# Attention's value products: two matmuls per key tile instead of three, and denominators from GpSimd sums

## The chip, the core and the metric

The kernel runs on one core of a Trainium2 chip. The core has a matrix engine (TensorE, called PE in the rows, with its weight loads as PEld), VectorE (DVE), ScalarE (ACT), GpSimd (POOL) and SyncE (SP, which issues DMAs). Each engine works through its own list of instructions in a fixed order. The metric is the time of one execution in microseconds; the profile shows one such execution, instruction by instruction.

## What is computed

One layer: a gated feed-forward block, then a mixer (attention beside a short convolution), then a second gated feed-forward block, for 1024 latent tokens and 256 context tokens with a model width of 1024. The change touches only the attention of the mixer, 8 query heads in 2 groups of 4 that share a key and value head of width 64:

```
def gqa_softmax(q, k, v):
    s = jnp.einsum('bqkgd,bskd->bkgqs', q, k, preferred_element_type=jnp.float32) * ATTN_SCALE
    p = jax.nn.softmax(s, axis=-1).astype(v.dtype)
    return jnp.einsum('bkgqs,bskd->bqkgd', p, v)
...
    k_all = jnp.concatenate([kc, k], axis=1)
    v_all = jnp.concatenate([vc, v], axis=1)
```

Every latent query reads 1280 keys: 1024 latent ones and 256 of the context. All inputs are float32.

## The kernel before

The program has three parts: the first feed-forward block with its loads (to about 770 us), the projections and attention (to about 1470 us), and the second feed-forward block. A scheduler puts every engine's instructions in order when the program is built, following the order of the code and the buffers that come free.

**Precision.** A float32 number is carried as a high part (rounded to the matrix engine's faster float32 type, `F32R`) and a low part, the rest. ACT writes the high part (a cast), DVE writes the low part (a subtraction of two tensors). A product of two such pairs is three matmuls: high by high, high by low, low by high.

**Attention.** The loop at L1564 goes over 16 pairs `gi` of a 128-query tile and a head group. For each of them `back` (L1403) goes over 10 key tiles `kt` of 128 keys. `st_exp` (L1325) makes one tile's scores for 4 heads x 128 queries (two matmuls into `pT`, L1330 and L1331) and their exponentials `pexp` (ACT, L1333). For the eight latent key tiles (`SPLIT`, L896) it then makes the high part (ACT, L1343) and the low part (DVE, L1344); for the two context tiles (`UNSPLIT`) it keeps the float32 tile. Three key tiles later (`LAG`, L1410) `tp_v` (L1347) multiplies by the values into a PSUM tile `pvo` of 128 rows: rows 0 to 63 are the sums of p times v, and rows 64 to 127 are the softmax denominator, since the right half of `v_hi` and `v_f` holds ones. A latent tile takes three matmuls (L1353, L1354, and L1355 with the low values from `vlq`, into 64 rows), and a context tile one float32 matmul (L1350), which the profile records as two matmuls.

After the tenth key tile `attn_end` (L1366) is stepped through during the next pair: ACT copies the denominators to `rcs` (L1372), DVE takes reciprocals (L1375) and multiplies (L1380), and squares are summed for the norm that follows.

**Beside it** run the steps of `front` for the next pair: score matmuls `s__` (L1307) whose row maxima DVE reduces out of PSUM (L1308), and `smax_end` (L1310), in which POOL makes a diagonal tile `dgm` (L1315) and copies queries (L1321). The fill generators `fill_pe` (L1258) and `fill_dve` (L1280) add the second half of the mixer's projections and the convolution's work in fixed proportions.

**Buffers.** Tiles tagged `t2` (128x512, six of them) hold `pexp`, some of the parts, and most temporaries. Three buffers tagged `raw` take weights from DMA until ACT and DVE have split them (L277). PSUM has 4 banks `in`, 3 banks `o` and 1 bank `m` (L88).

Of the kernel before, what the change touches and what calls it, by code (L numbers as in the profile page):

```python
# [6 lines left out]
F32 = mybir.dt.float32  # L7
# [20 lines left out]
def layer_kernel(  # L28
# [876 lines left out]
    def v_of(k):  # L905
        n = SPLIT.index(k)
        if k >= 8:
            return v_c[:, n - NVA, :, 0:P], v_c[:, n - NVA, :, P:P + HD]
        return vt["hi"][:, n], vt["lo"][:, n]

    vt = {}

# [59 lines left out]
    def make_v(pt, N, k0):  # L972
        vf = t2("vf", [P, N])
        act.copy(vf, pt)
        nt = N // P
        pv = ps("o", [P, nt, P], "pvt")
        for t in range(nt):
            pe.transpose(pv[:, t, :], vf[:, t * P:(t + 1) * P], ident)
        one = ones1.unsqueeze(2).to_broadcast([P, 2, HD])
        for t in range(nt):  # L980
            k = k0 + t
            src = pv[:, t, :].rearrange("p (g d) -> p g d", g=2)
            if k in SPLIT:
                v, vl = v_of(k)
                act.copy(v[:, :, 0:HD], src)
                dve.tensor_tensor(vl, src, v[:, :, 0:HD].bitcast(F32), op=ALU.subtract)
            else:
                v = v_f[:, UNSPLIT.index(k)]
                act.copy(v[:, :, 0:HD], src)
            act.copy(v[:, :, HD:P], one)  # L990

    def ctx_kv():
        kt_ = slot("XCb", [P, 2, 2, CTX], F32R, "kstc")
# [213 lines left out]
    vt["hi"] = slot("X1a", [P, NVA, 2, P], F32R, "v_hi")  # L1207
    NVL = NVA * 2 * HD
    vlq = wp.tile([P, NVL + 1024], F32R, tag="wu", name="vlq", bufs=5)
    vt["lo"] = vlq[:, 0:NVL].rearrange("p (s g d) -> p s g d", s=NVA, g=2)  # L1210
    k_proj(L0, 0, kf[0])
    v_proj(L0, 0)

# [111 lines left out]
    def st_exp(qt, g, qm, kt):  # L1325
        i, qc = qt // 4, (qt % 4) * P
        pt = ps("o", [P, 512], "pT")
        ks = kst[g] if kt < 8 else kst_cc[g]
        c = (kt if kt < 8 else kt - 8) * P
        pe.matmul(pt, ks[:, 0, c:c + P], qgrp(i, g, qc), start=True, stop=False)  # L1330
        pe.matmul(pt, ks[:, 1, c:c + P], qm, start=False, stop=True)  # L1331
        p = t2("pexp")
        act.activation(p, pt, AF.Exp)  # L1333
        if kt not in SPLIT:
            return p, None
        c = pn[0] % CY
        pn[0] += 1
        if c < 2:
            hi, lo = pbuf[:, 2 * c], pbuf[:, 2 * c + 1]
        else:  # L1340
            hi = t2("pth", dt=F32R)
            lo = t2("ptl", dt=F32R)
        act.copy(hi, p)  # L1343
        (pool if kt in POOLK else dve).tensor_tensor(lo, p, hi.bitcast(F32), op=ALU.subtract)  # L1344
        return hi, lo

    def tp_v(g, pv, kt, hl):  # L1347
        first, last = kt == 0, kt == NKT - 1
        if hl[1] is None:
            pe.matmul(pv, v_f[:, UNSPLIT.index(kt), g, :], hl[0], start=first, stop=last)  # L1350
        else:
            vh, vl = v_of(kt)
            pe.matmul(pv, vh[:, g, :], hl[0], start=first, stop=False)  # L1353
            pe.matmul(pv, vh[:, g, :], hl[1], start=False, stop=last)  # L1354
            pe.matmul(pv[0:HD], vl[:, g, :], hl[0], start=False, stop=last)  # L1355

    kg = []

# [7 lines left out]
    def attn_end(qt, g, pv):  # L1366
        i, qc = qt // 4, (qt % 4) * P
        if aT[i] is None:
            aT[i] = slot(("X0a", "X0b")[i], [P, 4, 512], F32, f"aT{i}")
        pvv = pv.rearrange("p (a e q) -> p a e q", a=2, e=2)  # L1370
        for e in range(2):
            act.copy(rcs[e * HD:(e + 1) * HD], pvv[HD:P, :, e, :])  # L1372
        yield
        for a in range(2):
            dve.reciprocal(rcs[:, a, :], rcs[:, a, :])  # L1375
# [1 line left out]
        dst = aT[i][:, 2 * g:2 * g + 2, qc:qc + P]  # L1377
        for e in range(2):
            r = slice(e * HD, (e + 1) * HD)
            dve.tensor_tensor(dst[r], pvv[0:HD, :, e, :], rcs[r], op=ALU.mult)  # L1380
        yield
        q = t2("asq", [P, 2, P])
        act.activation(q, dst, AF.Square)
# [451 lines left out]
```

## Time and profile before

| | us |
|---|---|
| median of 3 runs | 2164.17 (2163.52 to 2165.6) |
| the profiled execution | 2168.2, its span 2166.4 |
| attention: from the first key tile's exponentials to the last pair's end | about 1088 to 1425 |

| engine | busy over the span | busy between 1088 and 1425 us (337 us) |
|---|---|---|
| PE | 2130.6 us (98%) | 333.29 |
| DVE | 1546.3 us (71%) | 301.88 |
| ACT | 910.1 us (42%) | 249.54 |
| POOL | 227.6 us (11%) | 31.64 |

Read the busy time of PE with care. Matmuls are pipelined and the recorded end of one lies behind the start of the next, so a busy PE says only that it had something in flight; what a matmul costs is the distance from one start to the next. A duration of DVE or POOL includes any time in which the instruction had started and could not proceed.

### The profile page before, as it was taken

To read this page: it belongs to the slowest core of one execution; us is meant where nothing else is said; L and a number is where in the kernel's file an instruction comes from. 1 tells how busy PE (TensorE), PEld (TensorE's weight loads), DVE (VectorE), ACT (ScalarE), POOL (GpSimd) and SP (SyncE) were. 2 spreads that over 40 slices of the span, in tenths; PEclk is the share of its full clock that TensorE was granted. 3 is DMA by queue.
4 is the path that set the end of the run, shared out by engine and by line. 5 is a ranking of instruction groups with operands and counts; after the bars stand their busy time and mean duration, and the time that the engine had idled before them with its cause. 6 is when DMAs were issued, how large, how long until landed. Compare 5 with 4: busy or idle time off the path is not lost.

```text
span 2166.4 us, 26536 instructions
## 1 busy us (share of the span) xinstructions
PE 2130.6 (98%) x10084; PEld 1711.8 (79%) x10084; DVE 1546.3 (71%) x2109; ACT 910.1 (42%) x1415; POOL 227.6 (11%) x158
## 2 busy tenths in 40 slices
PE   8999999999999999999999999999999999999998
PEld 4788788888889887887777777777788888877877
DVE  5887776666657867661898899876866666668754
ACT  4422322222335533442567777754422232234433
POOL 0001111101010110000100100001011111123001
PEclk9999999999999999999999999999999999999998
DMA  8043344545379756342211101142232322378642
GB/s 323 16 146 127 124 147 138 167 130 170 127 242 341 263 178 228 119 136 68 88 49 30 40 20 68 49 151 73 78 99 101 117 94 91 107 287 283 225 147 78
DMA packets 111824, 296.01 MB, mean 137 GB/s; under 512 B 10704, under 2 KB 17872, under 8 KB 108624
## 3 DMA queue, kind: packets, MB, share of 16 engines
q1 hardware_dynamic: 111696, 294.32, 40.1%
q8 instruction: 79, 1.29, 0.2%
q14 instruction: 49, 0.40, 0.1%
HBM read 235.29 MB, written 56.36 MB: 135 GB/s over the span
## 4 chain that ended last, share of the span: by engine, by line
PE 75%; DVE 6%; DMA 4%; issue 2%; ACT 2%; POOL 0%; DVEq 0%; SPq 0%; ACTq 0%; POOLq 0%
PE p L508 9%; PE p L510 9%; PE p L509 9%; PE po L704 6%; PE po L706 6%; PE po L705 6%; DMA wa<-in_ada_dram 3%; PE pT L1331 1%; PE pT L1330 1%; PE pmo L1110 1%; PE pmo L1111 1%; PE pmo L1112 1%; PE pvo L1354 1%; PE pvo L1355 1%; PE pvo L1353 1%
## 5 line engine op out<-in xcount | busy, mean ns | idle before, releaser
L704 PE MATMUL po<-gst,wo 128*128 128x512 f32 (+1 forms) x636 | 248.4, 391 | 3.4 <-DVE x L667 3.4
L706 PE MATMUL po<-gst,wo 128*128 128x512 f32 (+1 forms) x636 | 247.2, 389 | 4.0 <-DVE wo L310 4.0
L705 PE MATMUL po<-gst,wo 128*128 128x512 f32 (+1 forms) x636 | 247.3, 389 | 0.0
L309 ACT CAST gst<-grt 128x1024 fp32r<-128x1024 f32 (+1 forms) x95 | 88.9, 936 | 218.7 <-PE po L706 96.4
L310 DVE TENSOR_TENSOR gst<-grt,gst 128x1024 fp32r<-128x1024 f32 (+1 forms) x95 | 110.6, 1165 | 73.7 <-ACT gst L309 73.5
L706 PEld LDWEIGHTS po<-gst,wo 128*128 128x128 f32 x636 | 120.0, 189 | 31.9 <-DVE wo L310 5.1
L704 PEld LDWEIGHTS po<-gst,wo 128*128 128x128 f32 x636 | 120.1, 189 | 31.5 <-issue 2.7
L705 PEld LDWEIGHTS po<-gst,wo 128*128 128x128 f32 x636 | 120.2, 189 | 26.4
L142 DVE SCALAR_TENSOR_TENSOR acc<-wa,cs,acc 128x1024 f32<-128x1024 f32 x70 | 90.5, 1314 | 60.3 <-DMA wa<-in_ada_dram 60.3
L508 PE MATMUL p<-h0h,wgA 128*128 128x512 f32 x320 | 126.6, 396 | 0.2 <-ACT e1f L528 0.2
L509 PE MATMUL p<-h0l,wgA 128*128 128x512 f32 x320 | 126.4, 395 | 0.0
L510 PE MATMUL p<-h0h,wgA 128*128 128x512 f32 x320 | 126.4, 395 | 0.0
L1333 ACT ACTIVATE pexp<-pT 128x512 f32<-128x512 f32 x160 | 94.5, 598 | 66.6 <-PE pT L1331 35.1
L309 ACT CAST wsB<-s 128x512 fp32r<-128x512 f32 x80 | 48.5, 620 | 152.9 <-DVE s L495 83.0
L277 DVE TENSOR_TENSOR wm<-wr,wm 128x1024 fp32r<-128x1024 f32 x52 | 64.8, 1249 | 42.3 <-ACT wm L273 42.0
L310 DVE TENSOR_TENSOR wo<-wr,wo 128x1024 fp32r<-128x1024 f32 x72 | 83.3, 1163 | 15.2 <-ACT wo L309 15.2
L310 DVE TENSOR_TENSOR wsA<-s,wsA 128x512 fp32r<-128x512 f32 x80 | 51.8, 687 | 54.3 <-ACT wsA L309 54.3
L309 ACT CAST wo<-wr 128x1024 fp32r<-128x1024 f32 x72 | 70.3, 976 | 27.2 <-DVE wr L628 16.1
L309 ACT CAST wuA<-wr 128x1024 fp32r<-128x1024 f32 (+1 forms) x40 | 33.5, 838 | 107.6 <-issue 58.7
L309 ACT CAST wsA<-s 128x512 fp32r<-128x512 f32 x80 | 45.6, 618 | 68.9 <-PE p L510 63.1
L508 PEld LDWEIGHTS p<-h0h,wgA 128*128 128x128 f32 x320 | 60.1, 188 | 14.6 <-ACT e1f L528 0.6
L510 PEld LDWEIGHTS p<-h0h,wgA 128*128 128x128 f32 x320 | 60.1, 188 | 14.5
(1077 smaller groups left out, 5966.8 us busy)
## 6 DMA issues: line engine op xcount, KB each, us to landing
wr<-in_wo_dram SPq DMA_DIRECT2D x92, 512.0 KB, 4.7
wr<-in_wi_dram SPq DMA_DIRECT2D x88, 512.0 KB, 3.7
wa<-in_ada_dram SPq DMA_DIRECT2D x56, 512.0 KB, 3.6
wr<-in_wmi_dram SPq DMA_DIRECT2D x38, 512.0 KB, 3.6
grt<-g1P SPq DMA_DIRECT2D x35, 512.0 KB, 4.8
grt<-g2P SPq DMA_DIRECT2D x35, 512.0 KB, 6.0
g1P<-ev SPq DMA_DIRECT2D x35, 256.0 KB, 3.2
g2P<-ev SPq DMA_DIRECT2D x35, 256.0 KB, 2.0
```

Of the source, the lines that this page charges most:

```text
L142: dve.scalar_tensor_tensor(acc[:, i, :], w, cs[:, j, k:k + 1], acc[:, i, :], op0=ALU.mult, op1=ALU.add)
L277: dve.tensor_tensor(w[:, 1, :], r, w[:, 0, :].bitcast(F32), op=ALU.subtract)
L309: act.copy(hi, t)
L310: dve.tensor_tensor(lo, t, hi.bitcast(F32), op=ALU.subtract)
L508: pe.matmul(pt, w[:, 0, c:c + P], hi, start=(k == 0 and not more), stop=False, skip_group_check=more)
L509: pe.matmul(pt, w[:, 0, c:c + P], lo, start=False, stop=False, skip_group_check=more)
L510: pe.matmul(pt, w[:, 1, c:c + P], hi, start=False, stop=(k == 3), skip_group_check=more)
L704: pe.matmul(o, wh, hi, start=st, stop=False, skip_group_check=g)
L705: pe.matmul(o, wh, lo, start=False, stop=False, skip_group_check=g)
L706: pe.matmul(o, wl, hi, start=False, stop=end, skip_group_check=g)
L1110: pe.matmul(pt, wh, hi[:, k, :], start=(i == 0), stop=False)
L1333: act.activation(p, pt, AF.Exp)
```

## The change

The values of a latent key tile lie as high and low halves side by side in one tile of 128 columns (`v_hi`), where the ones were before. One matmul with the high part of p writes the high product in rows 0 to 63 of `pvo` and the low product in rows 64 to 127; a second, into rows 0 to 63, multiplies the low part of p by the high values. The right half of the context values `v_f` becomes zeros. So `pvo` no longer holds the denominators. POOL adds up the ten `pexp` tiles of a pair into one of two accumulators (`accp`, a `raw` buffer), nine additions for each pair. `attn_end` spreads the sum over partitions with a float32 matmul against ones (`den`, in the one bank `m`). ACT copies `den` to `rcs` and the lower rows of `pvo` to a new tile `pvl`; DVE adds upper and lower rows and then multiplies by the reciprocal, one instruction more.

```
-        return vt["hi"][:, n], vt["lo"][:, n]
+        return vt["hi"][:, n]
...
-                dve.tensor_tensor(vl, src, v[:, :, 0:HD].bitcast(F32), op=ALU.subtract)
+                dve.tensor_tensor(v[:, :, HD:P], src, v[:, :, 0:HD].bitcast(F32), op=ALU.subtract)
...
-            act.copy(v[:, :, HD:P], one)
+            if k not in SPLIT:
+                act.activation(v[:, :, HD:P], ones1.unsqueeze(2).to_broadcast([P, 2, HD]), AF.Identity, scale=0.0)
...
-    vt["lo"] = vlq[:, 0:NVL].rearrange("p (s g d) -> p s g d", s=NVA, g=2)
+    accp = raw("accp")
+    psum_p = [accp[:, 512 * i:512 * i + 512] for i in range(2)]
...
         p = t2("pexp")
         act.activation(p, pt, AF.Exp)
+        acc = psum_p[(2 * qt + g) % 2]
+        if kt == 0:
+            p0[0] = p
+        else:
+            pool.tensor_tensor(acc, p0[0] if kt == 1 else acc, p, op=ALU.add)
...
-            pe.matmul(pv, v_f[:, UNSPLIT.index(kt), g, :], hl[0], start=first, stop=last)
+            pe.matmul(pv, v_f[:, UNSPLIT.index(kt), g, :], hl[0], start=False, stop=last)
         else:
-            vh, vl = v_of(kt)
-            pe.matmul(pv, vh[:, g, :], hl[0], start=first, stop=False)
-            pe.matmul(pv, vh[:, g, :], hl[1], start=False, stop=last)
-            pe.matmul(pv[0:HD], vl[:, g, :], hl[0], start=False, stop=last)
+            v = v_of(kt)
+            pe.matmul(pv, v[:, g, :], hl[0], start=first, stop=False)
+            pe.matmul(pv[0:HD], v[:, g, 0:HD], hl[1], start=False, stop=False, skip_group_check=True)
...
+        den = ps("m", [P, 512], "den")
+        pe.matmul(den, ones1.to_broadcast([P, P]), psum_p[(2 * qt + g) % 2], start=True, stop=True)
+        dnv = den.rearrange("p (a e q) -> p a e q", a=2, e=2)
+        pvl = t2("pvl", [P, 2, P])
         for e in range(2):
-            act.copy(rcs[e * HD:(e + 1) * HD], pvv[HD:P, :, e, :])
+            act.copy(rcs[e * HD:(e + 1) * HD], dnv[e * HD:(e + 1) * HD, :, e, :])
+            act.copy(pvl[e * HD:(e + 1) * HD], pvv[HD:P, :, e, :])
...
-            dve.tensor_tensor(dst[r], pvv[0:HD, :, e, :], rcs[r], op=ALU.mult)
+            dve.tensor_tensor(dst[r], pvv[0:HD, :, e, :], pvl[r], op=ALU.add)
+        dve.tensor_tensor(dst, dst, rcs, op=ALU.mult)
```

POOL's list, kernel before, from the second to the fifth pair of attention (`dgm` and the query copy into `vlq` belong to `smax_end`):

```order
L1315 TENSOR_TENSOR dgm<-cst,m_8681 128x512
L1315 TENSOR_TENSOR dgm<-cst,m_8878 128x512
L1321 TENSOR_SCALAR vlq<-qst_8074 64x512
L1315 TENSOR_TENSOR dgm<-cst,m_9110 128x512
L1321 TENSOR_SCALAR vlq<-qst_8074 64x512
```

The same stretch of POOL's list, changed kernel (each `accp` row is one addition of an exponential tile, x6 stands for six of them):

```order
L1316 TENSOR_TENSOR dgm<-cst,m_8676 128x512
L1339 TENSOR_TENSOR accp<-accp,pexp 128x512 x2
L1339 TENSOR_TENSOR accp<-pexp 128x512
L1339 TENSOR_TENSOR accp<-accp,pexp 128x512 x6
L1316 TENSOR_TENSOR dgm<-cst,m_8879 128x512
L1322 TENSOR_SCALAR vlq<-qst_8071 64x512
L1339 TENSOR_TENSOR accp<-accp,pexp 128x512 x2
L1339 TENSOR_TENSOR accp<-pexp 128x512
L1339 TENSOR_TENSOR accp<-accp,pexp 128x512 x6
```

Nine additions of 128x512 now stand in POOL's list for each pair, ahead of and behind the two instructions that were there.

PE's list, kernel before, where one pair's last context product is followed by the next pair's first latent products (`pq` is a projection from the fill):

```order
L1350 MATMUL pvo<-pexp,v_f 128x512
L1307 MATMUL s__8986<-kst,qst_8074 128x512
L1110 MATMUL pq<-h1h,wm 128x512
L1111 MATMUL pq<-h1l,wm 128x512
L1112 MATMUL pq<-h1h,wm 128x512
L1330 MATMUL pT<-qst_8074,kst 128x512
L1331 MATMUL pT<-vlq,kst 128x512
L1353 MATMUL pvo<-pbuf,v_hi 128x512
L1354 MATMUL pvo<-pbuf,v_hi 128x512
L1355 MATMUL pvo<-pbuf,vlq 64x512
```

PE's list, changed kernel, the same place at the end of the pair:

```order
L1356 MATMUL pvo<-pexp,v_f 128x512
L1377 MATMUL den<-accp,cst 128x512
L1308 MATMUL s__8994<-kst,qst_8071 128x512
L1110 MATMUL pq<-h1h,wm 128x512
L1111 MATMUL pq<-h1l,wm 128x512
L1112 MATMUL pq<-h1h,wm 128x512
```

and a latent tile's products there, with what stands around them:

```order
L1331 MATMUL pT<-qst_8071,kst 128x512
L1332 MATMUL pT<-vlq,kst 128x512
L1359 MATMUL pvo<-pth,v_hi 128x512
L1360 MATMUL pvo<-ptl,v_hi 64x512
L1110 MATMUL puu<-h1h,wm 128x512
```

`den` stands directly behind the pair's last context product and ahead of the next score matmuls, and the third matmul of a latent tile is gone.

## Rows read from the trace of the kernel before

**Rows 1.** Busy time in attention: us, PE, PEld, DVE, ACT, POOL, clock, DMA

```profile
1088.00:1425.00 337.00, 333.29 (x1441) 249.29 (x1440) 301.88 (x508) 249.54 (x430) 31.64 (x33) 1.00 0.13 44
```

**Rows 2.** The chain of work, part of attention: start us, us, what

```profile
1154.92 0.86 PE pvo L1350 x2
...
1159.88 0.23 PE pvo L1355
```

**Rows 3.** DVE's groups in attention: xcount | busy us, mean ns | idle before

```profile
L1344 DVE TENSOR_TENSOR ptl<-pexp,pth 128x512 fp32r<-128x512 f32 x64 | 48.7, 761 | 3.5 <-ACT pth L1343 3.0
L1344 DVE TENSOR_TENSOR pbuf<-pexp,pbuf 128x512 fp32r<-128x512 f32 x64 | 45.2, 711 | 2.7 <-ACT pbuf L1343 2.0
L1375 DVE RECIPROCAL rcs<-rcs 128x128 f32<-128x128 f32 x32 | 29.9, 939 | 0.1
L277 DVE TENSOR_TENSOR wm<-wr,wm 128x1024 fp32r<-128x1024 f32 x20 | 24.5, 1228 | 0.4 <-ACT wm L273 0.3
L1380 DVE TENSOR_TENSOR aT<-pvo,rcs 64x256 f32<-64x256 f32 x30 | 12.4, 412 | 0.3
```

**Rows 4.** Busy time in attention of line L1308 alone: us, DVE, clock, DMA

```profile
1088.00:1425.00 337.00, 102.52 (x177) 1.00 0.13 44
```

**Rows 5.** POOL's groups in attention

```profile
L1315 POOL TENSOR_TENSOR dgm<-cst,m 128x512 fp32r<-128x512 f32 x15 | 15.9, 1063 | 163.1 <-DVE m L1313 73.2 <-DVE ptl L1344 36.4 <-PE s__10997 L1307 18.5
L1321 POOL TENSOR_SCALAR vlq<-qst 64x512 fp32r<-64x512 f32 x14 | 10.1, 719 | 97.6 <-PE pT L1331 61.8 <-ACT pth L1343 18.4 <-DVE mx L1308 17.3
L949 POOL TENSOR_TENSOR qsw<-qsw,x1b 128x512 f32<-128x512 f32 x4 | 5.8, 1443 | 23.2 <-DMA qsw<-q 17.8 <-ACT pbuf L1343 5.3
```

**Rows 6.** Single lines: xcount: ns min/median/max, first and last start us

```profile
L949 POOL TENSOR_TENSOR qsw<-qsw,x1b x5: 1285/1288/1907, 1041.5 to 1245.5; 128x512 f32<-128x512 f32 x5
...
L1344 DVE TENSOR_TENSOR ptl<-pexp,pth x64: 627/682/2152, 1094.5 to 1417.3; 128x512 fp32r<-128x512 f32 x64
...
L574 DVE TENSOR_TENSOR sgc<-sgc,pc x20: 409/414/423, 131.3 to 630.1; 128x256 f32<-128x256 f32 x20
```

**Rows 7.** Timeline where POOL meets DVE: start us, us, instruction

```profile
1301.54 1.03 POOL L1315 TENSOR_TENSOR dgm<-cst,m 128x512 fp32r<-128x512 f32 x1
...
1301.64 1.48 DVE L1344 TENSOR_TENSOR ptl<-pexp,pth 128x512 fp32r<-128x512 f32 x1
...
1668.70 0.68 DVE L485 TENSOR_TENSOR s<-wr 128x512 f32<-128x512 f32 x1
...
1668.92 1.61 POOL L585 TENSOR_TENSOR gt<-e1f,ev 128x512 f32<-128x512 f32 x1 [16.94 <-DVE ev L579]
...
1669.42 1.66 DVE L486 TENSOR_TENSOR s<-s,wr 128x512 f32<-128x512 f32 x1
```

**Rows 8.** Timeline where POOL runs beside one-input and PSUM work of DVE

```profile
1232.52 1.29 POOL L949 TENSOR_TENSOR qsw<-qsw,x1b 128x512 f32<-128x512 f32 x1 [11.82 <-DMA qsw<-q]
...
1232.73 0.94 DVE L1375 RECIPROCAL rcs<-rcs 128x128 f32<-128x128 f32 x1
1233.60 0.63 DVE L1308 TENSOR_REDUCE mx<-s__9893 128x1 f32<-128x512 f32 x1
```

**Rows 9.** Timeline where POOL meets DVE work that leaves no gap

```profile
1508.13 4.81 POOL L486 TENSOR_TENSOR s<-s,wr 128x512 f32<-128x512 f32 x1 [11.51 <-ACT b L248]
...
1507.86 2.07 DVE L249 SCALAR_TENSOR_TENSOR b<-x,mod,b 128x512 fp32r<-128x512 f32 x3
...
1510.51 1.28 DVE L427 TENSOR_TENSOR t1f<-x,x 128x512 f32<-128x512 f32 x2
```

**Rows 10.** ACT's groups in attention

```profile
L1333 ACT ACTIVATE pexp<-pT 128x512 f32<-128x512 f32 x160 | 94.5, 598 | 66.6 <-PE pT L1331 35.1 <-DVE ptl L1344 12.1 <-PE pvo L1355 5.4
...
L1372 ACT COPY rcs<-pvo 64x256 f32<-64x256 f32 x32 | 11.8, 368 | 1.0 <-PE pvo L1350 0.4
```

**Rows 11.** Busy time in two short stretches, columns as in rows 1

```profile
40.00:50.00 10.00, 9.45 (x30) 3.20 (x28) 5.10 (x10) 5.35 (x12) 0.00 (x0) 1.00 0.67 274
...
1065.00:1070.00 5.00, 3.55 (x9) 2.53 (x10) 4.91 (x9) 3.64 (x6) 1.02 (x1) 0.71 0.00 0
```

More of the change, by code (lines that the diff above doesn't have):

```diff
@@ L978, in make_v @@
             pe.transpose(pv[:, t, :], vf[:, t * P:(t + 1) * P], ident)
-        one = ones1.unsqueeze(2).to_broadcast([P, 2, HD])
         for t in range(nt):
@@ L983, in make_v @@
             if k in SPLIT:
-                v, vl = v_of(k)
+                v = v_of(k)
                 act.copy(v[:, :, 0:HD], src)
-                dve.tensor_tensor(vl, src, v[:, :, 0:HD].bitcast(F32), op=ALU.subtract)
+                dve.tensor_tensor(v[:, :, HD:P], src, v[:, :, 0:HD].bitcast(F32), op=ALU.subtract)
             else:
```

## The prediction

> **What bounds the kernel now.** I read attention's stretch of the trace, 1088 to 1425 us, since the change touches nothing that runs long outside it. The busy times come first [rows 1]: of 337 us PE has something in flight for 333, DVE is busy for 302 (90%), ACT for 250, POOL for 32. The chain of waits then shows what PE's work costs from start to start: 0.23 us for a matmul of 128x512 in the faster float32 type, and 0.86 us for a float32 product, which is two records [rows 2]. It runs nearly all through PE there. So PE sets the pace now, and DVE has 337 - 302 = 35 us of idle time behind it. That is the margin to keep in mind: whoever gives DVE more than 35 us makes DVE the bound.
>
> The next view sorts DVE's work by what it reads. Row maxima out of PSUM take 102.5 us [rows 4], reciprocals 29.9 and the products out of PSUM 12.4 [rows 3]; some 15 us of small groups also read at most one tensor from SBUF. That makes 160 us. The remaining 142 us (up to 155, if the overlap of neighbours is given to the other side; I take 150) read two SBUF tensors: the low parts at L1344 (93.9 us) and the weights' low parts at L277 (24.5) above all [rows 3].
>
> The last view is the timeline at the places where POOL already works. A DVE subtraction that reads two SBUF tensors takes 0.68 us in the median [rows 6]; the one that met POOL's `dgm` took 1.48 and ended with it plus its own length. The same happens in the second feed-forward block: POOL's addition started under one DVE addition and took 1.61 instead of 1.29, because it waited for that one, and the next DVE addition took 1.66, because it waited for POOL [rows 7, 6]. One waits for the other in full; I found no pair that ran side by side. Work of DVE with one SBUF tensor or with PSUM is not touched: a reciprocal under a POOL operation of 1.29 us took its usual 0.94, and a reduction 0.63 [rows 8].
>
> **The change part by part.**
>
> PE loses 8 x 16 = 128 matmuls of 0.23 us, 29.4 us. It gains 16 float32 products `den`; the nearest row is the float32 product with the values, same shape, 0.86 us [rows 2], so 13.8 us. Net -15.6 us: PE would need 337 - 16 = 321 us if nothing else held it.
>
> POOL gains 9 x 16 = 144 additions of 128x512 in float32. The row is the same operation on the same shape, 1.285 us when undisturbed [rows 6]: 144 x 1.29 = 186 us. With the 32 it has [rows 5] POOL holds the shared path for 218 of 337 us.
>
> The Trainium skill, "GPSIMD Engine Reference", 3.1 Elementwise, puts a two-input element at about 2.6 cycles of 1.2 GHz; an estimate from it is 512 x 2.6 / 1.2 = 1.1 us, by which the additions would hold 160 us. The trace says 1.29 and decides. The same page, 4.1 Engine selection, speaks against the change: it gives elementwise additions to VectorE, as about twice as slow on GpSimd. On VectorE they would add 144 x 0.68 = 98 us to its queue by its own median [rows 6], so by that rule too DVE would be over its margin.
>
> DVE gains 16 multiplications of 128x256 with two SBUF inputs, 0.41 us each [rows 6], 6.6 us. The two out of PSUM per pair stay; only their second operand changes. The new load is the waiting. Two ends bound it.
>
> Lower end: two-input work of DVE and POOL's operations exclude each other, so the stage can't be shorter than their sum, 150 + 6.6 + 218 = 374 us (366 with 142). That is 29 to 37 us more than now, even if every POOL operation lay exactly over one-input work of DVE.
>
> Upper end: each addition costs DVE what it cost in the second feed-forward block, 1.66 - 0.68 = 0.98 us [rows 7]: 144 x 0.98 = 141 us.
>
> Value taken: this stage's own rows. L1344's 128 subtractions sum to 93.9 us [rows 3], and 128 x 0.681 = 87.2 would be undisturbed, so 6.7 us are waits, caused by 15 + 4 two-input operations of POOL [rows 5], 0.35 us for each. L1344 is some 87 of 150 us of such work, so over all of it 0.35 x 150/87 = 0.60. Those operations hold 1.09 us on average (15 x 1.03 and 4 x 1.29) against 1.29, so a little more: 0.65. 144 x 0.65 = 94 us.
>
> DVE then needs 302 + 94 + 7 = 403 us. It is now the bound, but it still waits now and then for a matmul or an exponential; of today's 35 us I leave a third, 12. The stage takes 415 us, 78 more than now. What PE saves is gone in this: it would be done in 321.
>
> Costed at nothing, with their cover. ACT's 32 copies of `pvl` are 32 x 0.368 = 11.8 us [rows 10], 262 of then 415 us. The new wait: `den` stands on PE behind the pair's last product and needs POOL's ninth addition; queued behind it are the next score matmuls, and so DVE's maxima and ACT's exponentials. The products lag three key tiles, some 6 us, so POOL may be four additions late before PE waits. Holding `pexp` until POOL has read it keeps one of six `t2` buffers longer, and ACT's next exponential waits for it; ACT waits 12 us for DVE's low parts already [rows 10]. One of three `raw` buffers is lost, but in this stage only 20 weight tiles pass [rows 3], one in 17 us. If these covers fail, the upper end's 47 us is my allowance for all of them together. What `make_v` saves lies ahead of the stage; zero.
>
> The clock: PE would work some 321 of 415 us. A stretch with 30 matmuls in 10 us, fewer than that, shows a granted clock of 1.00; one around an idle of over 2 us on PE shows 0.71 [rows 11]. Gaps of the new kind are below 1 us each, so I take 1.00.
>
> Sum: 2168.2 (profiled execution) + 78 - 4 (the median lies 4.0 below it) = 2242; I say 2240.
>
> **The rivals.**
>
> *Perfect nesting.* POOL's additions fall over the maxima and reciprocals, and DVE hardly waits. For it: the order alternates L1344 with one or two maxima. Against it: a reduction is 0.6 us and an addition 1.29, so most stick out. Time: the lower end, +29 to +37, about 2197.
>
> *Full waits and a late sum.* Each addition costs 0.98 us, or POOL falls behind and PE stands at `den`. For it: the repeated pattern of [rows 7]. Against it: half of DVE's work here is not touched. 302 + 141 + 7 + 12 = 462, +125: about 2289.
>
> *POOL gives way, faster.* Where DVE's two-input work leaves no gap, POOL's addition waited through it (4.81 us for 1.29 of work) and DVE's operations kept their lengths [rows 9]. If the additions lived on such leftovers alone, PE would stay the bound: 2168.2 - 16 - 4 = 2148. This decides only if POOL finds 218 us in DVE's idle and one-input time, which is 35 + 152 = 187 of 337, or 171 of the 321 that it would have. It doesn't fit, unless the two can share the path in a way that no row shows.
>
> **How the numbers follow.** Forecast (+50 to +105): 0.65. Perfect nesting: 0.13. Full waits or worse: 0.15. POOL gives way: 0.04; something that cancels to within the 0.2% (about 4 us) that a measurement of this kernel tells from no change: 0.03. Range 2192 to 2300, from the lower end of the sum to a little over the upper one. Faster 0.04, same 0.03, slower 0.93.
>
> **What would show it.** Right: in attention's stretch DVE busy near 97%, POOL at 50% or more with additions of 1.3 to 2 us, L1344's mean at 1.0 us or more from 0.74, maxima unchanged at 0.68, PE's idle time ended by DVE, the stage some 410 us long, everything after it shifted and unchanged. Wrong: L1344 still near 0.7 us beside additions of 1.3 (no exclusion); PE's waits led by `den` on POOL (a late sum, not DVE); a granted clock below 1.00 in the stage; or a change outside attention.

## The result: slower by 3.7%

The changed kernel takes 2244.51 us (2241.66 to 2250.93), the kernel before, run beside it, 2164.89 us (2163.52 to 2168.45). The ratio is 1.0366, with a 95% interval of 1.0348 to 1.0384. The prediction said 2240 us in a range of 2192 to 2300, and slower with a chance of 0.93.

The profiled execution took 2247.08 us with a span of 2244.9 us, 78.5 more than before. Attention, from the start of the first exponential to the end of the last product with the values, takes 406.4 us instead of 332.9, which is 73.5 of the 78.5. The stage starts 2.5 us later. From its end to the first matmul of the second feed-forward block's main loop (L508) it is 106.6 us instead of 105.0, and from there to the end 640.0 instead of 639.0. So nearly the whole loss is made in attention, and the rest of the program is only shifted.

Between the two feed-forward blocks the busy times read as follows in the kernel after (columns: stretch, its length, PE, PEld, DVE, ACT, POOL, granted clock, DMA share, GB/s). It is the row that answers to [rows 1]:

```profile
1091.00:1498.00 407.00, 350.16 (x1325) 233.80 (x1324) 389.75 (x516) 254.98 (x457) 247.76 (x177) 0.95 0.10 33
```

DVE is now busy for 96% of the stretch, up from 90%, and POOL for 61% instead of 9%. PE has something in flight for 86%, where it had 99%. The bound has moved from PE to DVE. The same stretch for the maxima alone (line L1309, which was L1308) shows the same work in the same time as [rows 4], 102.37 for 102.52 us:

```profile
1091.00:1498.00 407.00, 102.37 (x177) 0.95 0.10 33
```

DVE's groups (count | busy us, mean ns | idle before), which answer to [rows 3]; L1350 was L1344, L1385 was L1375:

```profile
L1350 DVE TENSOR_TENSOR ptl<-pexp,pth 128x512 fp32r<-128x512 f32 x64 | 74.8, 1168 | 3.5 <-PE pvo L1359 1.3 <-ACT pth L1349 1.3 <-issue 0.4
L1350 DVE TENSOR_TENSOR pbuf<-pexp,pbuf 128x512 fp32r<-128x512 f32 x64 | 71.4, 1121 | 5.0 <-ACT pbuf L1349 4.7
L277 DVE TENSOR_TENSOR wm<-wr,wm 128x1024 fp32r<-128x1024 f32 x18 | 28.4, 1577 | 0.0
L1385 DVE RECIPROCAL rcs<-rcs 128x128 f32<-128x128 f32 x30 | 27.6, 930 | 0.2 <-ACT rcs L1381 0.2
L1391 DVE TENSOR_TENSOR aT<-aT,rcs 128x256 f32<-128x256 f32 x15 | 16.1, 1073 | 0.2
L1390 DVE TENSOR_TENSOR aT<-pvo,pvl 64x256 f32<-64x256 f32 x30 | 12.3, 411 | 0.3
```

Whatever reads two tensors from SBUF in these groups has grown: L1350 from a mean of 0.74 to 1.14 us, L277 from 1.23 to 1.58, and the new multiplication takes 1.07 where its shape alone takes 0.41 [rows 6]. The reciprocals (one input) and the new additions out of PSUM kept their 0.93 and 0.41 us.

POOL's largest groups in the same stretch, and two lines of the view of the tile `accp` (the second says who waited for it: us, times). They answer to [rows 5]:

```profile
L1339 POOL TENSOR_TENSOR accp<-accp,pexp 128x512 f32<-128x512 f32 x128 | 190.1, 1485 | 95.5 <-ACT pexp L1334 91.5
L1339 POOL TENSOR_TENSOR accp<-pexp 128x512 f32<-128x512 f32 x16 | 23.1, 1444 | 45.1 <-ACT pexp L1334 45.1
...
L1339 POOL TENSOR_TENSOR accp<-accp,pexp x128: 1262/1428/2267, 1095.6 to 1495.6; 128x512 f32<-128x512 f32 x128
...
  ACT rcs L1381: 2.7, 5
```

The shortest addition takes 1.26 us and the mean 1.48. POOL still has idle time before the additions, and nearly all of it ends with the next exponential: POOL keeps up. Only ACT's copy waits a little for what hangs on the sum, 2.7 us in all; nothing is listed as waiting for a `pexp` tile that an addition still holds.

The timeline of a piece of the stage shows the mechanism, POOL first and then DVE (start us, us, instruction):

```profile
1296.29 4.04 POOL L1339 TENSOR_TENSOR accp<-accp,pexp 128x512 f32<-128x512 f32 x2 [0.32 <-ACT pexp L1334]
1300.30 1.71 POOL L1339 TENSOR_TENSOR accp<-pexp 128x512 f32<-128x512 f32 x1
...
1296.99 2.21 DVE L277 TENSOR_TENSOR wm<-wr,wm 128x1024 fp32r<-128x1024 f32 x1
1299.24 1.65 DVE L1192 TENSOR_TENSOR qst<-q,qst 64x512 fp32r<-64x512 f32 x1
1300.91 0.69 DVE L1309 TENSOR_REDUCE mx<-s__10244 128x1 f32<-128x512 f32 x1
1301.52 0.68 DVE L1309 TENSOR_REDUCE mx<-s__10247 128x1 f32<-128x512 f32 x1
```

VectorE's two-input instructions and the additions take turns. L277 starts during the first addition and takes 2.21 us instead of its mean of 1.23 before. The second addition ends at 1300.33, 1.13 us after L277, which is about its own length, so the two additions last 4.04 us instead of 2.6. L1192 is issued at 1299.24 and ends 0.56 us after that second addition. The third addition then runs under two maxima out of PSUM, and these take their usual 0.69 and 0.68.

The whole stage does the same. Worked out from the rows of L1350: 87 of its 128 subtractions have their turn while a GpSimd instruction runs, and 78 of these end 0.55 us after it (to within 0.03 us). In the kernel before there were 11 such meetings, of which 9 end that way.

PE waits for DVE now. Four of the longest waits of ACT and PE in the stage (engine and what waited <- what it waited for: us in all, times, longest); the third is one for POOL, to which the experiments come back:

```profile
ACT pexp L1334 <- DVE ptl L1350: 20.2, 13, 3.5
...
PEld pvo L1360 <- DVE ptl L1350: 17.1, 17, 2.1
PEld pm L1319 <- POOL dgm L1316: 15.3, 12, 3.4
...
PEld pvo L1360 <- DVE pbuf L1350: 11.5, 14, 2.5
```

### The profile page after: what moved, and what is told of

Same layout as the page of the kernel before. It is cut to its first block, busy times and chain, and to the rows that moved or that the text cites. A ratio compares the mean times of both kernels' runs of the same rounds, so it can differ in the third digit from the quotient of the medians.

```text
span 2244.9 us, 26697 instructions
## 1 busy us (share of the span) xinstructions
PE 2152.7 (96%) x9988; PEld 1700.7 (76%) x9988; DVE 1639.8 (73%) x2125; ACT 916.8 (41%) x1439; POOL 445.7 (20%) x302
## 5 line engine op out<-in xcount | busy, mean ns | idle before, releaser
L1339 POOL TENSOR_TENSOR accp<-accp,pexp 128x512 f32<-128x512 f32 x128 | 190.1, 1485 | 95.5 <-ACT pexp L1334 91.5
L508 PE MATMUL p<-h0h,wgA 128*128 128x512 f32 x320 | 126.8, 396 | 1.0 <-ACT ev L528 0.5
L277 DVE TENSOR_TENSOR wm<-wr,wm 128x1024 fp32r<-128x1024 f32 x52 | 69.9, 1345 | 59.5 <-ACT wm L273 58.4
L1350 DVE TENSOR_TENSOR ptl<-pexp,pth 128x512 fp32r<-128x512 f32 x64 | 74.8, 1168 | 3.5 <-PE pvo L1359 1.3
L1350 DVE TENSOR_TENSOR pbuf<-pexp,pbuf 128x512 fp32r<-128x512 f32 x64 | 71.4, 1121 | 5.0 <-ACT pbuf L1349 4.7
```

Source lines behind the costliest of these rows:

```text
L508: pe.matmul(pt, w[:, 0, c:c + P], hi, start=(k == 0 and not more), stop=False, skip_group_check=more)
L1339: pool.tensor_tensor(acc, p0[0] if kt == 1 else acc, p, op=ALU.add)
```

## The experiments

To compare stages I split VectorE's time in attention into three: waiting (what an instruction takes beyond the median length that its operation and shape have in the trace before), its own work (the rest of its busy time), and idle time. All are worked out from every VectorE row between the first exponential and the last value product; the three add up to the stage within 1 us. Where instructions overlap, part of a wait lies under the instruction in front, so that own work comes out some 6 us low where the waiting is large: the changed kernel has 6.6 us more of it than the kernel before, though the table shows the same. Each ratio is taken against the kernel before as it ran beside that kernel.

The scheduler orders every kernel anew. The order of VectorE's and PE's instructions is the changed kernel's in e2 and e5, almost the changed kernel's in e1, and almost that of the kernel before in e4 (at most 0.3% of the list stands elsewhere). In the others more has moved, and the text says so where it matters.

| kernel | us | ratio to before [95%] | stage | own | waiting | idle |
|---|---|---|---|---|---|---|
| before | 2164.9 | | 332.9 | 287.9 | 10.7 | 35.1 |
| after | 2244.5 | 1.0366 [1.0348, 1.0384] | 406.4 | 287.9 | 101.1 | 17.2 |
| e1_no_adds | 2168.0 | 1.0006 [0.9997, 1.0015] | 330.1 | 291.6 | 13.5 | 25.5 |
| e4_adds_only | 2236.7 | 1.0319 [1.0305, 1.0333] | 399.3 | 283.6 | 89.2 | 26.7 |
| e2_half_adds | 2193.2 | 1.0132 [1.0116, 1.0147] | 357.6 | 288.9 | 46.7 | 22.0 |
| e5_one_input | 2184.3 | 1.0095 [1.0081, 1.0109] | 346.3 | 289.1 | 35.4 | 21.7 |
| e7_lo_from_psum | 2201.1 | 1.0171 [1.0156, 1.0186] | 364.4 | 288.0 | 52.2 | 24.0 |
| e3_dve_adds | 2241.4 | 1.0343 [1.0329, 1.0357] | 406.6 | 371.2 | 8.7 | 27.2 |
| e6_ones_column | 2174.0 | 1.0035 [1.0023, 1.0048] | 336.8 | 294.2 | 12.5 | 31.0 |
| e8_short_reciprocal | 2175.4 | 1.0056 [1.0043, 1.0069] | 338.3 | 274.8 | 10.8 | 52.7 |
| e9_no_reciprocal | 2161.2 | 0.9974 [0.9959, 0.9988] | 323.4 | 268.7 | 13.2 | 41.4 |
| e10_no_spread | 2155.0 | 0.9946 [0.9929, 0.9962] | 321.3 | 290.0 | 10.9 | 21.0 |
| e12_own_tile | 2163.2 | 0.9987 [0.9976, 0.9998] | 326.6 | 289.8 | 14.4 | 22.3 |
| e11_dma_spread | 2184.3 | 1.0078 [1.0050, 1.0106] | 343.4 | 313.7 | 10.8 | 18.8 |

### Which part of the change costs the time

**e4_adds_only**: the kernel before, with the additions put in and their sums unused.

```
         act.activation(p, pt, AF.Exp)
+        acc = psum_p[(2 * qt + g) % 2]
...
+            pool.tensor_tensor(acc, p0[0] if kt == 1 else acc, p, op=ALU.add)
```

> The kernel before with the 144 additions on GpSimd put in, and nothing read from their sums; the three matmuls per key tile stay. Theory: VectorE's own 299 us in the stage plus 144 x 0.65 = 94 us of waiting plus some 15 us idle = 408 against 334, so +74: 2238 us (2222 to 2252). Rival (late sum: TensorE waits at den): den is not there, so near 2165 to 2180. Rival (the new end of a pair): 2165.

Measured: 2236.7 us, and 89 us of waiting in VectorE. The additions alone make 70 of the 80 us, with PE's three products per key tile still in place. The other 10 were not taken apart; the new two-input multiplication (L1391, 16.1 us in the changed kernel) belongs to what e4 doesn't have.

**e1_no_adds**: the changed kernel without them (the accumulators hold ones).

```
+    dve.memset(accp, 1.0)
...
-            pool.tensor_tensor(acc, p0[0] if kt == 1 else acc, p, op=ALU.add)
```

> The changed kernel with the 144 additions on GpSimd left out: the accumulator is filled with ones once, so the denominators are constants and the output is not attention's. Everything else of the change stays (two matmuls per key tile, den, pvl, the extra multiplication). Theory (GpSimd's additions and VectorE's two-tensor work exclude each other): nothing of the loss is left, attention is bound by TensorE again and 16 us shorter than before: 2149 us (2145 to 2156). Rival (the new end of a pair, den, its bank and the copies, costs the time): most of the loss stays, 2200 us or more. Rival (the lower granted clock by itself): the same 2149, since TensorE would be busy again; this run does not tell it from the theory.

Measured: 2168.0 us, the time of before. The loss is gone with the additions, as the theory and the rival of the clock both had it, but the gain expected from PE's 16 us is not there. That miss is taken up below. The low parts, without GpSimd's additions beside them:

```profile
L1346 DVE TENSOR_TENSOR ptl<-pexp,pth 128x512 fp32r<-128x512 f32 x64 | 46.5, 727 | 5.2 <-ACT pth L1345 3.7 <-issue 0.7 <-PE pvo L1355 0.3
L1346 DVE TENSOR_TENSOR pbuf<-pexp,pbuf 128x512 fp32r<-128x512 f32 x64 | 44.4, 699 | 5.1 <-ACT pbuf L1345 4.6
```

### Is it mutual exclusion

The theory: while a GpSimd instruction runs, no VectorE instruction with two SBUF inputs does. A rival: the accumulations' dependences and buffers (a `pexp` held longer) slow the chain. A second: POOL comes late with `dgm`, which stands in its list among the additions. By the distances from one matmul start to the next, PE loses 12.7 us in front of `pm`, which needs `dgm`, but 8.1 of these are there in e1 too, so the additions make some 5 us of it. A third: the lower granted clock (0.95 in the stage). In e2, e5 and e7 the stage's granted clock is 1.00, as in e1, and they are still 16 to 33 us slower than e1.

**e2_half_adds**: the same 144 additions on the same tiles, but on 256 of the 512 columns (half of the sum is left out).

```
+    dve.memset(accp, 1.0)
...
+            h = slice(0, 256)
-            pool.tensor_tensor(acc, p0[0] if kt == 1 else acc, p, op=ALU.add)
+            pool.tensor_tensor(acc[:, h], (p0[0] if kt == 1 else acc)[:, h], p[:, h], op=ALU.add)
```

> The changed kernel with additions of 256 columns instead of 512 (the other half of the accumulator is constant, so half of the denominators are not attention's). Same number of additions, same waits, half the time for which GpSimd holds the path: 0.73 us each from 1.29, by the row of a 256-column product in the kernel before. Theory: waiting of VectorE per addition falls with the holding time, from 0.63 to 0.2 to 0.36 us (a maximum of 0.6 us can hide most of it), so the stage is 21 to 52 us longer than without additions (330): 2189 to 2220 us. Rival (number of additions, buffers held until GpSimd has read them, a late sum): 2235 to 2245.

Measured: 2193.2 us. The additions and the low parts:

```profile
L1341 POOL TENSOR_TENSOR accp<-accp,pexp x128: 722/742/2400, 1095.0 to 1446.3; 128x256 f32<-128x256 f32 x128
...
L1352 DVE TENSOR_TENSOR ptl<-pexp,pth 128x512 fp32r<-128x512 f32 x62 | 56.3, 908 | 4.1 <-issue 2.2 <-ACT pth L1351 1.3
```

The instructions, their order and the tiles that they hold are unchanged; only the additions' length fell, to 0.74 us in the median, and the waiting fell from 101 to 47 us. So the length counts, not the number of additions. A shorter addition also gives its buffers back sooner; this run alone doesn't rule that rival out.

**e5_one_input**: GpSimd writes p + 1 instead of the sum, which reads one tensor.

```
-            pool.tensor_tensor(acc, p0[0] if kt == 1 else acc, p, op=ALU.add)
+            pool.tensor_scalar(acc, p, 1.0, 1.0, op0=ALU.mult, op1=ALU.add)
```

> The changed kernel with GpSimd instructions that read one tensor (p + 1 into the accumulator) in place of the additions, 128x512 as before; the denominators are not sums. By the query copy's row such an instruction holds 0.61 us. Theory, exclusion with every GpSimd instruction: as with half additions or a little less, 2185 to 2210. Theory, exclusion only between two-tensor instructions on both sides: as without additions, 2162 to 2175, with the low parts' subtraction near 0.74 us. Rival (buffers held, late sum): 2235 to 2245.

Measured: 2184.3 us, just under the range given for exclusion by every GpSimd instruction and far from no effect. GpSimd's group and the low parts (columns as above):

```profile
L1339 POOL TENSOR_SCALAR accp<-pexp 128x512 f32<-128x512 f32 x143 | 106.7, 746 | 174.0 <-ACT pexp L1334 171.6
...
L1350 DVE TENSOR_TENSOR ptl<-pexp,pth 128x512 fp32r<-128x512 f32 x64 | 54.5, 851 | 4.6 <-POOL accp L1339 1.5 <-ACT pth L1349 1.4 <-issue 1.2
L1350 DVE TENSOR_TENSOR pbuf<-pexp,pbuf 128x512 fp32r<-128x512 f32 x64 | 50.5, 793 | 3.9 <-ACT pbuf L1349 3.4
```

The operation takes 0.62 us in the median and 0.75 on average, and L1350's means are 0.85 and 0.79 against 0.73 and 0.70 without it (e1). Of the 50 subtractions that have their turn while a GpSimd instruction runs, 36 end 0.55 us after it (to within 0.03 us). A GpSimd instruction with one input excludes VectorE's two-input work as well; it only does so for a shorter time.

Over the three lengths the waiting above e1's 13.5 us is 22 us at 0.62, 33 at 0.74 and 88 at 1.29 us per instruction: 0.15, 0.23 and 0.61 us for each of 144. It grows faster than the length. A likely reason, not tested by itself: a short one finds room beside a maximum of 0.68 us, while one of 1.29 always sticks out.

**e7_lo_from_psum**: the low part is taken from the exponential's input tile in PSUM instead of `pexp`, so that L1350 reads one tensor from SBUF (the low parts are then of the scores, not of the exponentials).

```
-        (pool if kt in POOLK else dve).tensor_tensor(lo, p, hi.bitcast(F32), op=ALU.subtract)
+        dve.tensor_tensor(lo, pt, hi.bitcast(F32), op=ALU.subtract)
```

> The changed kernel with all additions on GpSimd, but VectorE's 128 subtractions of the low parts read the scores in PSUM instead of the exponentials in SBUF, so each has one SBUF tensor; the low parts are wrong. Their order and what they wait for (the high part) stay; scores stay in PSUM some 1.3 us longer. Theory: these subtractions no longer meet GpSimd and are back at 0.68 us; of 101 us of waiting in VectorE 58 lay on them, so the stage is 50 to 60 us shorter than in the changed kernel: 2189 us (2180 to 2205). Rival (late sum, buffers, lower clock): no change, 2240 to 2250.

Measured: 2201.1 us, in the range. POOL's additions, then DVE's groups:

```profile
L1339 POOL TENSOR_TENSOR accp<-accp,pexp 128x512 f32<-128x512 f32 x121 | 167.5, 1384 | 98.3 <-ACT pexp L1334 95.3
...
L1350 DVE TENSOR_TENSOR pbuf<-pT,pbuf 128x512 fp32r<-128x512 f32 x62 | 41.7, 679 | 1.8 <-ACT pbuf L1349 1.4
L1350 DVE TENSOR_TENSOR ptl<-pT,pth 128x512 fp32r<-128x512 f32 x61 | 41.7, 683 | 8.2 <-ACT pth L1349 6.3 <-POOL accp L1339 1.2 <-issue 0.2
L277 DVE TENSOR_TENSOR wm<-wr,wm 128x1024 fp32r<-128x1024 f32 x17 | 28.1, 1655 | 0.1
```

With one operand moved to PSUM the subtractions are back at 0.68 us while the additions run, and the line that still reads two SBUF tensors, L277, waits as much as in the changed kernel. 87 subtractions again have their turn while a GpSimd instruction runs, and 4 of them end 0.55 us after it, where it was 78 in the changed kernel. This separates the two kinds of VectorE work within one kernel. The rival of buffers and dependences does not explain it: the additions read and wrote the same tiles. The run is not quite a change of one thing, since 3 to 4% of the lists of PE, VectorE and ACT stand in another order. And with VectorE out of the way a buffer wait does appear: ACT's exponentials wait 11.6 us for additions that still hold a tile.

The Trainium skill, "GPSIMD Engine Reference", 8 Key points, says that GpSimd shares its SBUF interfaces with VectorE, with contention against VectorE instructions that have two SBUF inputs or run in a 2-port performance mode. The runs agree with the first condition and put a size to it, since the operations wait for each other's whole length; no run here shows the second.

### Would the additions be better elsewhere

**e3_dve_adds**: the additions on VectorE.

```
-            pool.tensor_tensor(acc, p0[0] if kt == 1 else acc, p, op=ALU.add)
+            dve.tensor_tensor(acc, p0[0] if kt == 1 else acc, p, op=ALU.add)
```

> The changed kernel with the same additions on VectorE instead of GpSimd. Theory: no exclusion left, but VectorE has 144 x 0.62 = 89 us of own work more: 288 own + 11 waits for the two GpSimd instructions that stay + 7 + 89 = 395, plus 12 to 17 idle = 407 to 412, stage as long as in the changed kernel: 2246 us (2232 to 2256), with the low parts' subtraction back at 0.74 us from 1.14. If the loss came from holding the exponentials for GpSimd or from a late sum rather than from VectorE's queue: clearly below, 2190 or less.

Measured: 2241.4 us. The additions and the low parts on VectorE:

```profile
L1339 DVE TENSOR_TENSOR accp<-accp,pexp 128x512 f32<-128x512 f32 x125 | 87.8, 702 | 4.7 <-ACT pexp L1334 4.4
L1350 DVE TENSOR_TENSOR ptl<-pexp,pth 128x512 fp32r<-128x512 f32 x63 | 44.3, 703 | 0.4 <-ACT pth L1349 0.3
L1350 DVE TENSOR_TENSOR pbuf<-pexp,pbuf 128x512 fp32r<-128x512 f32 x64 | 43.9, 686 | 3.0 <-ACT pbuf L1349 2.8
```

VectorE's own work rises by 83 us and its waiting falls to 9. On GpSimd the same additions cost VectorE 88 us of waiting. In this stage moving an addition to GpSimd relieved VectorE of nothing. (The order differs from the changed kernel's in 9% of VectorE's list.) The Trainium skill, "GPSIMD Engine Reference", 4.1 Engine selection, gives such additions to VectorE as about twice as fast; the instruction is (0.70 against 1.48 us here), but the kernel's time is the same within 0.3%.

**e6_ones_column**: no additions. The low values keep 63 of their 64 columns and the last one holds ones (the low part of one channel in 64 is left out), so that row 127 of `pvo` sums p times one; the low parts' product gets the whole 128 columns again, so that it adds the low parts of p to that row. ACT copies the lower rows, a matmul with a selecting column spreads row 127, and VectorE's addition of upper and lower rows masks it out (0.48 us instead of 0.41).

```
-                dve.tensor_tensor(v[:, :, HD:P], src, v[:, :, 0:HD].bitcast(F32), op=ALU.subtract)
+                dve.tensor_tensor(v[:, :, HD:P - 1], src[:, :, 0:HD - 1], v[:, :, 0:HD - 1].bitcast(F32), op=ALU.subtract)
...
+            act.copy(v[:, :, P - 1:P], ones1.unsqueeze(2).to_broadcast([P, 2, 1]))
...
+        pe.matmul(den, ident[HD:P, P - 1:P].to_broadcast([HD, P]), pvs[HD:P], start=True, stop=True)
```

> A version without any sum on an elementwise engine: the value tile of a key tile holds 64 high columns, 63 low columns and one column of ones, both matmuls use it with all 128 columns, so row 127 of the product is the denominator; a float32 matmul with a selecting column spreads that row. It leaves out the low part of one of the 64 value channels of each head group. Theory: TensorE saves 128 x 0.23 and adds 16 x 0.86, VectorE gets 16 x 0.41 = 7 us and has 35 idle, GpSimd nothing: 2149 us (2145 to 2158). If den with its waits and copies costs more than its own time: 2160 or more.

Measured: 2174.0 us, 0.35% above before and 25 us above the expectation. The sums can be had without the 144 additions for some 6 us over e1, but the rest of the change still brings no gain.

### Why PE's 16 us do not show

PE's own time in attention (each matmul at its usual distance to the next) is 323.0 us before and 306.6 after, and in e1: 16.4 less, as predicted. But what the starts stand further apart than that rises from 19.8 us before to 35.2 in e1 (111.5 in the changed kernel; some starts also stand closer than usual, so that the two don't add up to the stage). PE's saving comes back as waits. In e1 the largest are at the matmul `pm` (8.1 us, for POOL's `dgm`) and the score matmuls (5.0), the others are spread. Before, `pm` had 2.1. Five runs looked for what makes them. In e9, e10 and e12 the scheduler put other instructions elsewhere too: 1 to 5% of PE's list and 4 to 12% of VectorE's, against e1. What the order by itself is worth was not measured, so a difference of a few microseconds need not come from what was left out.

**e8_short_reciprocal** (on e6): reciprocals of 128x4 instead of 128x128 twice, with four small matmuls and four transposes for each pair.

```
-        pe.matmul(den, ident[HD:P, P - 1:P].to_broadcast([HD, P]), pvs[HD:P], start=True, stop=True)
...
+            pe.matmul(den[:, h:h + 1], pvs[HD:P, h * P:(h + 1) * P], ident[HD:P, P - 1:P], start=True, stop=True)
+        rden = tp.tile([P, 4], F32, tag="rden", name="rden", bufs=2)
+        dve.reciprocal(rden, den)
...
+            pe.transpose(rb[:, h * P:(h + 1) * P], rden[:, h:h + 1].to_broadcast([P, P]), ident)
```

> The version with the column of ones, with VectorE relieved: the denominators of a pair are brought to 128 queries x 4 heads by four small matmuls, the reciprocal is taken of 128x4 instead of two of 128x128, and four transposes spread it again. It leaves out the low part of one of 64 value channels. VectorE loses 32 x 0.94 = 30 us and gains 16 x 0.17 = 3; TensorE trades the float32 matmul of 0.86 us for small ones of about the same sum. If the missing 16 us of TensorE's saving were lost to VectorE's load (own work and waits 305 of 330 us without additions), the stage falls to about 320: 2154 us (2148 to 2162), below the kernel before. If they are lost to something else (waits at den, copies, the clock): 2165 to 2176 as with the long reciprocals.

Measured: 2175.4 us, no better than e6. VectorE lost 19 us of work, and its idle time rose by 22. But PE's own time rose by 7 (306.4 to 313.4), so the run moved two things at once. e9 moves one.

**e9_no_reciprocal** (on e1): no reciprocals at all (what is multiplied is the denominator).

```
-        for a in range(2):
-            dve.reciprocal(rcs[:, a, :], rcs[:, a, :])
-            yield
+        yield
+        yield
```

> The kernel without the additions (the accumulators hold ones), and with the 32 reciprocals of the denominators left out too: what is multiplied is the denominator, not its inverse. VectorE loses 32 x 0.86 = 27.6 us of the stage against the run without additions, and its queue a 0.86 us step twice a group; no other engine's work changes. If VectorE's load is what keeps TensorE's 16 us from showing, the time falls from 2168 to about 2152. If the 16 us are lost in waits of the engines for each other that no single engine's load makes, it stays at 2162 to 2169.

Measured: 2161.2 us, 7 below e1, just under the range given to hand-overs and 9 above that of VectorE's load. The waits at `pm` fall from 8.1 to 1.7 us. So without the reciprocals about 7 of the 16 us come back; whether by VectorE's load, by the step that they are between a pair's products and its end, or by the order is not told apart.

**e10_no_spread** (on e1): no float32 matmul `den`; the copies read the ones.

```
-        den = ps("m", [P, 512], "den")
-        pe.matmul(den, ones1.to_broadcast([P, P]), psum_p[(2 * qt + g) % 2], start=True, stop=True)
+        den = psum_p[(2 * qt + g) % 2]
```

> The kernel without the additions and without the float32 matmul that spreads the sums (the copies read the ones from SBUF). TensorE loses another 16 x 0.86 = 13.8 us against the run without additions, VectorE and GpSimd nothing. If TensorE's own work sets the stage's pace, the time falls from 2168 to about 2154. If the pace is set by the hand-overs between engines, so that TensorE's work taken away comes back as waits, it stays above 2161.

Measured: 2155.0 us, 13.0 below e1, of 13.8 taken from PE. Here PE's time comes back nearly in full. So the stage has not simply stopped depending on PE. It is not PE's time alone that the run takes away, though: ACT's copies no longer wait for `den`, and the one bank `m`, which `den` shares with `pm`, is free. The run also says more of the 128 products. Against the kernel before it has these products less and no `den`: 29.4 us of PE's work is gone, and some 12 us of the time (ratio 0.9946, 8 to 15 us by its interval), with the new copies and the multiplication in place. So the products taken out between the key tiles gave back some four tenths of what they cost, and `den` then took about as much again: that is how e1 comes out at the time of before.

**e12_own_tile** (on e1): `pvl` lies in a tile of its own instead of one of the six `t2` buffers.

```
-    psum_p = [accp[:, 512 * i:512 * i + 512] for i in range(2)]
+    psum_p = [accp[:, 0:512]] * 2
+    pvl = accp[:, 512:768].rearrange("p (a q) -> p a q", a=2)
...
-        pvl = t2("pvl", [P, 2, P])
```

> The kernel without the additions, with the copy of the low half (pvl) in a tile of its own instead of one of the six rotating ones that the exponentials, their high and their low parts share. No instruction is added or taken away. If the tile held over two steps is what ate TensorE's 16 us: 2152 to 2157 against 2168. If it was not: 2164 to 2170.

Measured: 2163.2 us, 5 below e1 and just under what was given for no effect; by the ratios to before the two differ by 0.2%, which is the limit of what can be told. The buffer held over two steps, or the order, may cost a few microseconds, not the 16.

**e11_dma_spread** (on e6): the row of sums goes through memory to all partitions, ACT and GpSimd issuing the transfers, and no spreading matmul is left. The reciprocals are also cut otherwise, as 64x256 instead of 128x128.

```
...
+        act.dma_start(dd, pvs[P - 1:P])
         yield
+        pool.dma_start(dn, dd.to_broadcast([P, 512]))
...
+            dve.reciprocal(rcs[e * HD:(e + 1) * HD], dnv[e * HD:(e + 1) * HD, :, e, :])
```

> The ones-column kernel (no additions; the low values' last column replaced by ones, which leaves out the low part of one channel in 64) with the spread taken off TensorE: ACT writes the row of denominators to memory, GpSimd's queue reads it back to all partitions, and the copy and the row lie in a tile of their own. Against the ones-column kernel (2174) TensorE loses 16 x 0.86 = 13.8 us and ACT 32 short copies, 12 us. If TensorE's work at the group's end sets the pace, as the run without the spread suggests: 2160; if the tile held out of the rotation was also in the way: 2150. If the row comes late through memory, VectorE waits at the reciprocals 16 times for 1 us or more: 2175 or above.

Measured: 2184.3 us, slower than e6, but not for the reason given: VectorE waits only 0.6 us for the transfers. The reciprocals show it:

```profile
L1388 DVE RECIPROCAL rcs<-keep 64x256 f32<-64x256 f32 x30 | 52.3, 1743 | 1.0 <-DMA keep<-dend 0.6
...
1088.00:1430.00 342.00, 319.33 (x1289) 227.77 (x1288) 322.70 (x505) 239.96 (x409) 42.08 (x48) 0.98 0.15 49
```

Half as many partitions with twice the columns took 1.74 us each instead of 0.93, so VectorE got 24 us more while PE lost 14. VectorE is busy for 94% of that stretch. As a test of the spread it is inconclusive, since the edit moved two costs at once.

What stays open: e9 and e12 each won back a part (7 and 5 us); whether the two add up was not tried, and the rest is spread over many small waits for which no single cause was shown. Only e9, e10 and e12 are below the kernel before, and each leaves out work that the result needs. No version was found that beats it.

## Why the prediction was right, step by step

- **DVE as the new bound: right.** The margin of 35 us was overrun. DVE is busy for 96%, where 97% was forecast, and the waits of PE for L1350 lead its list.
- **Exclusion: right, and shown** by e2, e5 and e7 and by the ends of the subtractions, not only by [rows 7]. That POOL's one-input instructions hold the path too is in the sum (the 32 us of [rows 5] are in the 218) and holds (e5).
- **0.65 us of waiting for each addition, 94 us: right.** Waiting rose from 10.7 to 101.1 us, so 90 us or 0.63 each. The stage's own rows were the better base: the second feed-forward block's 0.98 would have given 141. L1350 carries 58.2 of the 101 us, 58%, which is the share (87 of 150) by which its waits had been scaled up. That the number came so close is in part luck. Its base is ten subtractions that were held up, 6.7 us in all, two of them also behind a one-input copy, which the prediction doesn't count there; and 0.60 scaled in proportion to the additions' length is 0.71, not 0.65, which would have made it 2250.
- **Idle time left, a third of 35: about right.** 17.2 us instead of 12. The stage grew by 73.5 us instead of 78; 5 more fell outside it, where nothing had been forecast.
- **PE's -15.6 us: right as work, wrong as time.** PE's own time fell by 16.4 us. The forecast did not need the saving, but the third rival did: its 2148 took PE's saving as given once the additions cost nothing, and e1 shows 2168. The reading behind it, that PE alone sets the pace while DVE has 35 us in hand, was too simple: of the products' 29.4 us only some 12 show in e10. That a saving in the middle of a chain of hand-overs is partly lost fits this, but no single cause was shown.
- **The covers at zero: mostly right.** The sum is not late (2.7 us of waits behind `den`), and ACT, with its new copies, is busy for 255 of the 407 us. POOL's lateness with `dgm`, some 5 us of waits, is not among the covers. Holding a `t2` buffer may cost up to 5 us (e12), only visible where the additions are gone.
- **The clock at 1.00: wrong, with little effect.** The mean over the stretch is 0.95, and the prediction had named a clock below 1.00 as a sign of being wrong. The step that failed is "gaps of the new kind are below 1 us each": PE's weight loads wait up to 3.4 us for `dgm`, and there are stretches of 2 us without a matmul. Four pieces of 2 us, one after the other (columns as in [rows 1]):

```profile
1348.00:1350.00 2.00, 0.00 (x0) 0.00 (x0) 2.00 (x1) 0.00 (x0) 1.56 (x2) 1.00 0.00 0
1350.00:1352.00 2.00, 1.83 (x5) 1.34 (x6) 2.00 (x4) 0.60 (x1) 1.05 (x1) 0.59 0.00 0
1352.00:1354.00 2.00, 2.00 (x6) 1.18 (x4) 2.00 (x4) 1.75 (x4) 0.23 (x1) 0.56 0.00 0
1354.00:1356.00 2.00, 2.00 (x10) 1.58 (x9) 2.00 (x2) 0.35 (x2) 1.54 (x1) 1.00 0.00 0
```

PE does nothing for 2 us while DVE and POOL work, then runs for most of 4 us at the lower of its two levels, 1.2 GHz (a mean of 0.59 and 0.56 of full speed, 5 and 6 matmuls in 2 us), and then at the upper one, 2.4 GHz (10 matmuls). DVE is busy through all four, so the slower matmuls cost it no time here. Over the whole stage DVE idles for 17.2 us, which bounds what slower matmuls can have cost.

- **The rivals.** Perfect nesting (2197) did not come: the stage is 32 us longer than the sum of what excludes each other (374). Full waits (2289) did not come either: 0.63, not 0.98 us each. POOL does not give way: its additions take 1.48 us on average, not 4.81 as in [rows 9]. A change outside attention, which would have spoken against the forecast, is there but small (5 us).

## What to carry to other kernels

Before giving GpSimd elementwise work, count VectorE's instructions with two SBUF inputs in that stage and its idle time: the GpSimd time that does not fall beside one-input or PSUM work is taken from VectorE, and here an addition cost VectorE as much on GpSimd as on VectorE itself. Where such work must stay, moving one operand to PSUM frees it, and shorter GpSimd instructions cost less than in proportion. A matmul taken out between steps that hand tiles to each other may give back much less than its length (here some 12 of 29.4 us), while leaving out one at a pair's end gave back 13.0 of 13.8: do not price a saving by its length alone, and test it by itself.

## What was not expected of the hardware

- A GpSimd instruction with one input tensor (0.62 us) holds VectorE's two-input work off like one with two (e5: L1350 at 0.82 us on average against 0.71 without).
- The waiting per GpSimd instruction is not proportional to its undisturbed length: 0.15, 0.23 and 0.61 us at 0.62, 0.74 and 1.29 us.
- A reciprocal of 64x256 takes 1.74 us and one of 128x128 0.93, with the same number of elements: here the time goes with the columns.
